# Four borders between stages of a two-block transformer: where gate products, a side projection and two sums stand, and one bank more

## The chip, the cores and the metric

One core of one Trainium2 chip runs the whole program. The metric is the device time of one execution in microseconds (us). TensorE (PE) multiplies matrices, VectorE (DVE) and ScalarE (ACT) do elementwise work, SyncE (SP) issues the weight transfers, GpSimd (POOL) does little here. Each engine runs its own queue of instructions in order and waits at an instruction until what that needs is there.

## What is computed

256 tokens of width 1024 pass two blocks. The first has a layer with gated linear attention (GLA) and one with stick-breaking attention, each with a squared-ReLU MLP and layer norms. The second has two layers of a mixed attention (forgetting and retention heads), a gated convolution FFN and a gated side input p. What the change touches, cut from the reference:

```python
q, k, v, g, a1 = jnp.split(x @ w_in, ...)                 # GLA mixer
log_a = jax.nn.log_sigmoid((a1 @ w_a2 + b_a)) / GATE_TAU   # its gates
b = jnp.cumsum(to_chunks(log_a), axis=3)
...
h = layer_norm(DEEPNORM_ALPHA * h + sq_relu_mlp(...), ...)  # end of the first block
u = rms_norm(h, attn_norm_w[i])                            # second block, i = 0, 1
...
u = rms_norm(h, ple_norm_w[i])
h = h + jax.nn.sigmoid(u @ w_ple_gate[i]) * (p[i] @ w_ple_proj[i])
...
return rms_norm(h, final_norm_w)
```

## The kernel before

All activations lie with the model width on the 128 partitions (8 blocks of 128) and the 256 tokens along the row. The products are float32 by two halves: a weight is split into a rounded part wh (ACT, L330) and a rest wl (DVE, L333), an activation into x0 and x1, and `mm3` writes three matmuls for one product, L402, L403 and L404, with 256 or 512 columns. In the trace x0, x1 and h are all called b, since they come from one pool of large tiles.

Weights stream through: `prep` writes one chunk of 128x1024 (512 KB), its transfer on SP into one of 4 buffers `raw`, its cast on ACT and its subtraction on DVE into one of 6 pairs wh, wl. Products accumulate in PSUM banks of two pools: `up` has 3 banks, `acc` 4, and one bank `aux` is for sums and spreads. A tile that takes a bank again waits until the last reader of the bank is done. Pools for small tiles (`sq`, `lnq`, `pleg`) have few buffers and wait in the same way.

The order of each queue is set when the program is built: a scheduler takes the instructions of all engines by priority, which follows the order in which the code is written, and by its own estimate of when each is ready. What is written later goes behind, casts of later weights slip in between, and the chip runs the queues as they then stand.

The four places of the change:

- The gates of GLA. `gla` projects v in two halves of 48 matmuls (`w_gv`, j = 0 and 1, 16 steps of three). `hooks` are pairs of a step and a function that is called there. `rank` (step 11 of the first half) makes the low rank a1 by 16 matmuls, then ACT and DVE split it (L755, L756, tile a). `gates` (step 14) multiplies it by w_a2 into two `acc` banks (8 matmuls, L764), then takes the log-sigmoid and the running sums: four ABS on ACT (L768), four DVE operations (L769), Exp and Ln over all (L396), a subtraction (L773), four scans (L775), a subtraction (L777), the rows `glagrow`, twelve `glaE` (L808), and `glaK`, `glaQ` (L819, L822), which the first GLA product (L829) needs. Between them PE has the second half of v and the q and k projections (`w_gqk`).
- The p projections. `ple_proj` makes both products with p, one per layer, between the last layer norm's sums and its application. Each has four blocks in an `up` bank, and each block has a copy to SBUF on ACT (L1243) and, at the end, a transfer to a DRAM buffer `prd`. The second one's blocks have six matmuls of 512 columns. `normed` then applies the norm: per pair of blocks lnq (DVE L618), h (L624), x0 (ACT L626), x1 (DVE L627), and squares on ACT with a running sum `ssum` on DVE (L642, L644).
- The first layer's gate (`ple`, L1249 to L1269). Four blocks of `w_pg0`; the last is done in two halves, (0,) and (1,), which lie in one bank. DVE multiplies each by the norm's factor (L1266), ACT takes the sigmoid, DVE multiplies by p's part (L1268) and adds h (L1269). Behind it come the squares for the next norm (L526, L527, L642), the projections w_rg and w_f of the next layer, with the sums over the partitions (L486, which needs ssum), the reciprocal root by Ln and Exp (rsv, rsa, rsr) and its spread over the tokens (diag, L495, and four matmuls L496).
- The last layer (`last`). `w_pg1` in 16 steps; at step 3 `stat` asks for the two sums (L486 and the root behind it), at step 7 `turn(1)` transposes the second half of h.

Of the kernel before, what the change touches and what calls it, by code (L numbers as in the profile page):

```python
# [10 lines left out]
F32 = mybir.dt.float32  # L11
F32R = mybir.dt.float32r
# [3 lines left out]
P = 128  # L16
T = 256
D = 1024
KB = D // P
# [194 lines left out]
KST, KSS, KPL, KRM, KSP = 5, 5, 1, 7, 3  # L214
# [5 lines left out]
class Net:  # L220
# [511 lines left out]
    def gla(self, x):  # L732
        nc = self.nc
# [54 lines left out]

        v = self.b8().rearrange("p a b -> p (a b)").rearrange("p (c n) -> p c n", c=2)
        for j in range(2):  # L790
            pv = self.proj_tok("w_gv", j, x, hooks=[(11, rank), (14, gates)] if j == 0 else ())
            for c in range(2):
                after = nc.scalar.copy(v[:, c, j * 512:(j + 1) * 512], pv[c].rearrange("p a b -> p (a b)")).ins
        dep = mybir.DependencyInfo(mybir.DependencyClass.NoSync, mybir.DependencyReason.DATA)
# [418 lines left out]
                prev = hid  # L1213
        return self.late(accs, lambda c: self.down(accs, nm, j0, prev, pn, False, True, [c]))

    def ple_proj(self, stats):

        nc = self.nc
        self.prd = []
        for l in range(2):  # L1220
            pr = self.b8()
            pt = self.t([P, 2, T], "ptin")
            i = nc.scalar.dma_start(pt, self.A["p"][l]).ins
            self.tc.add_manual_dep(i, self.mark.name, mybir.DependencyInfo(mybir.DependencyClass.NoSync, mybir.DependencyReason.DATA), reason="order")
            px = (self.t([P, 2, T], "ph", F32R), self.t([P, 2, T], "pl", F32R))
            self.split(px, slice(0, 2), pt)
            w, _ = self.w(f"w_pp{l}", 0)
            halves = self.ready[self.use - 1][2]
            for c in range(4):
                ps = self.pup()  # L1230
                if l == 0:
                    for i in range(2):
                        for k in range(2):
                            self.mm3(ps[:, i, :], *w((2 * c + i) * 2 + k), px[0][:, k, :], px[1][:, k, :],
                                     k == 0 and i == 0, k == 1)
                else:
                    cs, ns = slice(c // 2 * P, c // 2 * P + P), slice(c % 2 * 512, c % 2 * 512 + 512)
                    for k in range(2):
                        self.mm3(ps.rearrange("p a b -> p (a b)"), px[0][:, k, cs], px[1][:, k, cs],
                                 *(t[:, ns] for t in halves[k]), k == 0, k == 1)  # L1240
                if l == 0 and c == KPL:
                    stats()
                nc.scalar.copy(pr[:, 2 * c:2 * c + 2, :], ps)  # L1243
            d = self.dram.tile([P, 8, T], F32, name=f"prd{l}")
            nc.scalar.dma_start(d, pr)
            self.prd.append(d)

    def ple(self, l, h, x, acc):
        nc = self.nc  # L1249
        n = self.b8()  # L1250
        pr = self.b8()
        nc.scalar.dma_start(pr, self.prd[l])
        for c in range(4):
            w, _ = self.w(f"w_pg{l}", c)
            ps = self.pup()
            g = self.t([P, 2, T], "pleg")
            for os in (((0, 1),) if c < 3 else ((0,), (1,))):
                for k in range(KB):
                    for o in os:
                        self.mm3(ps[:, o, :], *w(2 * k + o), x[0][:, k, :], x[1][:, k, :], k == 0 and o == 0, k == KB - 1)  # L1260
                    if c == 0 and k == KRM:
                        R2 = self.rms_full(acc).unsqueeze(1).to_broadcast([P, 2, T])
                a, b = os[0], os[-1] + 1
                sl = slice(2 * c + a, 2 * c + b)
                gg = g[:, a:b, :]
                nc.vector.tensor_tensor(out=gg, in0=ps[:, a:b, :], in1=R2[:, a:b, :], op=ALU.mult)  # L1266
                self.act(gg, gg, "Sigmoid")
                nc.vector.tensor_tensor(out=gg, in0=gg, in1=pr[:, sl, :], op=ALU.mult)  # L1268
                nc.vector.tensor_tensor(out=n[:, sl, :], in0=gg, in1=h[:, sl, :], op=ALU.add)  # L1269
        return n  # L1270


    def last(self, h, x, acc):
        nc = self.nc
# [47 lines left out]
                q.dma_start(self.out[c * P:(c + 1) * P, i * 512:i * 512 + 512], yy)  # L1322

        turn(0)
        ps = self.proj_tok("w_pg1", 0, x, hooks=[(3, stat), (7, lambda: turn(1))])
        for c in range(2):
            leave(c, 0, 0, 512, flat(ps[c]), 3 * c)
        self.w("w_pg1", 2)
# [18 lines left out]
    def run(self):  # L1347
# [31 lines left out]
        for l in range(2):  # L1379
# [8 lines left out]
            ln = self.layer_norm(h, mix, f"ln_g{l}1", f"ln_b{l}1", l == 0)  # L1388
            if end(f"b{l}", lambda: (ln['stats'](), self.normed(ln))[1][0]):
                return  # L1390
        self.ple_proj(ln["stats"])
        h, x, acc = self.normed(ln, "an0")
        for l in range(2):
            if l == 1:
                x, acc = self.rms(h, f"an{l}")
            o, hooks = self.mix2(l, x, acc)
            h = self.residual(h, self.pairs(f"w_out{l}", o, hooks, 6))
            if end(f"c{l}", lambda: h):
                return
            x, acc = self.rms(h, f"fn{l}")  # L1400
            h = self.residual(h, self.ffn2(l, x, acc))
            if end(f"d{l}", lambda: h):
                return
            x, acc = self.rms(h, f"pn{l}")
            if l == 1:
                return self.last(h, x, acc)
            h = self.ple(l, h, x, acc)
            if end(f"e{l}", lambda: h):
                return
# [28 lines left out]
```

## Time and profile before

| | us |
|---|---|
| median of 3 runs | 1303.39 (1301.37 to 1304.65) |
| the profiled execution, own time | 1302.13 |
| its span | 1300.4 |
| PE busy in it | 1282.7 (99%) |
| DVE, ACT busy | 946.8 (73%), 750.8 (58%) |
| TensorE's granted clock, mean | 0.998 |

The span is what the profiler sees from the first to the last instruction; the rest of an execution lies around it. A row of a timeline gives the start, the length, the engine, the line, the operation with its output and inputs, and, in brackets, how long the engine was idle before it and what ended that. A run of equal instructions stands in one row with its count (x4), and the length is then that of the run. The ends of matmuls are modelled, so the pitch from start to start tells more than the length.

### The profile page before, as it was taken

Reading aid. Unit: us, or ns where it says so; the run is one execution under the profiler, and the core shown is the slowest. Engines: PE = TensorE matmul, PEld = TensorE weight load, DVE = VectorE, ACT = ScalarE, POOL = GpSimd, SP = SyncE. Lnnn points to the kernel's source line nnn. Section 1 sums busy time; section 2 is a strip of 40 time slices with the busy share of each in tenths; the row PEclk is TensorE's granted clock in tenths of the full one; section 3 lists DMA queues with packets and bytes.
Section 4 is the critical chain, followed back from the end, with each engine's and each line's share of the span. In section 5 each row is a group of like instructions: output and inputs, shape, how many; then the busy total and the mean of one; then the engine's idle time right before and its main releaser. Section 6 shows DMA issues by size and latency. Waiting matters only on the chain.

```text
span 1300.4 us, 25420 instructions
## 1 busy us (share of the span) xinstructions
PE 1282.7 (99%) x10314; PEld 1236.5 (95%) x10314; DVE 946.8 (73%) x1514; ACT 750.8 (58%) x1181; POOL 36.2 (3%) x89
## 2 busy tenths in 40 slices
PE   8999999999999999999999999999999999999997
PEld 6999999999899999999989999999989899999996
DVE  6979855559557955558887788766787869885755
ACT  6556744447776744446746665544674557554544
POOL 0000000000231000000010000000001000000000
PEclk9999999999999999999999999999999999999999
DMA  8654666654533575555654465565657446656561
GB/s 288 217 172 155 193 197 183 189 179 141 185 115 118 171 228 189 185 189 194 215 182 140 138 207 187 183 184 158 220 167 221 141 127 196 192 185 188 170 222 50
DMA packets 64694, 232.78 MB, mean 179 GB/s; under 512 B 7216, under 2 KB 7488, under 8 KB 63936
## 3 DMA queue, kind: packets, MB, share of 16 engines
q1 hardware_dynamic: 61920, 220.75, 54.1%
q10 hardware_dynamic: 2016, 8.28, 1.7%
q0 software_dynamic: 640, 2.11, 0.5%
q8 instruction: 81, 1.33, 0.4%
q14 instruction: 37, 0.30, 0.1%
HBM read 227.96 MB, written 3.16 MB: 178 GB/s over the span
## 4 chain that ended last, share of the span: by engine, by line
PE 90%; DVE 5%; DMA 3%; ACT 2%; issue 1%; POOL 0%; SPq 0%; POOLq 0%; ACTq 0%; DVEq 0%
PE up L402 20%; PE up L403 19%; PE up L404 19%; PE acc L403 9%; PE acc L404 8%; PE acc L402 8%; DVE wl L333 1%; DMA raw<-in_w_pg_dram 1%; PE aux L976 1%; ACT wh L330 1%; DMA wa<-in_w_a_dram 1%; PE aux L586 1%; PE acc L1128 1%; PE acc L1070 0%; DMA raw<-in_w_gv_dram 0%
## 5 line engine op out<-in xcount | busy, mean ns | idle before, releaser
L333 DVE TENSOR_TENSOR wl<-raw,wh 128x1024 fp32r<-128x1024 f32 (+2 forms) x420 | 506.3, 1210 | 257.1 <-ACT wh L330 255.4
L330 ACT CAST wh<-raw 128x1024 fp32r<-128x1024 f32 (+2 forms) x420 | 434.9, 1036 | 387.3 <-PE acc L403 139.2
L402 PE MATMUL up<-b,wh 128*128 128x256 f32 (+1 forms) x2032 | 576.2, 284 | 2.8 <-DVE pleg L1266 1.6
L403 PE MATMUL up<-b,wh 128*128 128x256 f32 (+1 forms) x2032 | 572.4, 282 | 0.2 <-DVE b L527 0.2
L404 PE MATMUL up<-b,wl 128*128 128x256 f32 (+1 forms) x2032 | 569.6, 280 | 0.0
L402 PEld LDWEIGHTS up<-b,wh 128*128 128x128 f32 x2032 | 381.5, 188 | 10.3 <-issue 5.2
L403 PEld LDWEIGHTS up<-b,wh 128*128 128x128 f32 x2032 | 382.8, 188 | 1.2 <-DVE b L527 0.4
L404 PEld LDWEIGHTS up<-b,wl 128*128 128x128 f32 x2032 | 382.9, 188 | 0.2 <-issue 0.2
L403 PE MATMUL acc<-b,wh 128*128 128x256 f32 (+1 forms) x960 | 270.6, 282 | 0.0
L404 PE MATMUL acc<-b,wl 128*128 128x256 f32 (+1 forms) x960 | 270.4, 282 | 0.0
L402 PE MATMUL acc<-b,wh 128*128 128x256 f32 (+1 forms) x960 | 270.2, 281 | 0.0
L402 PEld LDWEIGHTS acc<-b,wh 128*128 128x128 f32 x960 | 181.1, 189 | 0.1
L403 PEld LDWEIGHTS acc<-b,wh 128*128 128x128 f32 x960 | 181.0, 189 | 0.1
L404 PEld LDWEIGHTS acc<-b,wl 128*128 128x128 f32 x960 | 180.7, 188 | 0.1
L402 PE MATMUL up<-wh,b 128*128 128x512 f32 (+1 forms) x136 | 52.9, 393 | 1.6 <-ACT wh L361 1.6
L403 PE MATMUL up<-wl,b 128*128 128x512 f32 (+1 forms) x136 | 51.9, 381 | 0.0
L404 PE MATMUL up<-wh,b 128*128 128x512 f32 (+1 forms) x136 | 51.7, 381 | 0.0
L467 ACT CAST b<-ffny 128x256 fp32r<-128x256 f32 x44 | 17.9, 407 | 54.3 <-DVE ffny L1202 53.4
L402 PEld LDWEIGHTS up<-wh,b 128*128 128x128 f32 x136 | 25.5, 188 | 8.2 <-ACT wh L361 2.3
L404 PEld LDWEIGHTS up<-wh,b 128*128 128x128 f32 x136 | 25.5, 188 | 5.3
L403 PEld LDWEIGHTS up<-wl,b 128*128 128x128 f32 x136 | 25.6, 188 | 4.9 <-DVE wl L362 0.4
L1194 DVE TENSOR_TENSOR glaS<-up,rfr 128x256 f32<-128x256 f32 x44 | 18.7, 425 | 12.4 <-PE up L404 12.3
(257 smaller groups left out, 1151.3 us busy)
## 6 DMA issues: line engine op xcount, KB each, us to landing
raw<-in_w_fu_dram SPq DMA_DIRECT2D x88, 512.0 KB, 4.2
raw<-in_w_mu_dram SPq DMA_DIRECT2D x64, 512.0 KB, 4.1
raw<-in_w_md_dram SPq DMA_DIRECT2D x64, 512.0 KB, 4.2
raw<-in_w_fd_dram SPq DMA_DIRECT2D x32, 512.0 KB, 3.7
raw<-in_w_sqk_dram SPq DMA_DIRECT2D x16, 512.0 KB, 4.1
raw<-in_w_rqk_dram SPq DMA_DIRECT2D x16, 512.0 KB, 4.9
raw<-in_w_fqk_dram SPq DMA_DIRECT2D x16, 512.0 KB, 4.4
raw<-in_w_out_dram SPq DMA_DIRECT2D x16, 512.0 KB, 3.8
```

The source lines that it names most:

```text
L330: i = nc.scalar.copy(hi, r).ins
L333: i = nc.vector.tensor_tensor(out=lo, in0=r, in1=hi, op=ALU.subtract).ins
L402: mm(o, wh, xh, start=first, stop=False, skip_group_check=True)
L403: mm(o, wh, xl, start=False, stop=False, skip_group_check=True)
L404: self.last_mm = mm(o, wl, xh, start=False, stop=last, skip_group_check=True).ins
L467: nc.scalar.copy(out[0][:, i, :], src)
L586: nc.tensor.matmul(ps[:, k, :], ones, s[k][:, i, :], start=(k == 0 and i == 0), stop=(i == 1), skip_group_check=True)
L976: self.nc.tensor.matmul(pO[r, i // 2, :], v[:, 0, hc], ws[i][:, 0:256], start=(i < 2), stop=False, skip_group_check=True)
L1128: mm(pls[i][:, a:b], qk[r, 0, a:a + P], qk[r, 1, 0:b - a], start=(a == 0), stop=True, skip_group_check=True)
L1194: nc.vector.tensor_tensor(out=a[:, 2:], in0=ps[:, 0, :], in1=R, op=ALU.mult)
```

## The change

Four edits, all of where something is written or which bank it takes; no product, sum or transfer is added or left out. `gates` moves from step 14 of the first half of v to step 1 of the second, nine matmuls later. `ple_proj` is cut into `ple_load` (transfer, split, weights) and `ple_proj` (products, copies, transfer out), and the second projection's part is written behind `normed`. The last half block of `ple` takes an `acc` bank instead of the second half of the `up` bank. In `last` the sums are asked for at step 10 instead of step 3.

```diff
-            pv = self.proj_tok("w_gv", j, x, hooks=[(11, rank), (14, gates)] if j == 0 else ())
+            pv = self.proj_tok("w_gv", j, x, hooks=[(11, rank)] if j == 0 else [(1, gates)])
...
-    def ple_proj(self, stats):
...
-        for l in range(2):
-            pr = self.b8()
...
+    def ple_load(self, l):
+        nc = self.nc
+        pr = self.b8()
...
+        return l, pr, px, w, halves
+
+    def ple_proj(self, l, pr, px, w, halves, stats=None):
+
+        nc = self.nc
+        if l == 0:
+            self.prd = []
+        for c in range(4):
+            ps = self.pup()
...
+            nc.scalar.copy(pr[:, 2 * c:2 * c + 2, :], ps)
+        d = self.dram.tile([P, 8, T], F32, name=f"prd{l}")
+        nc.scalar.dma_start(d, pr)
+        self.prd.append(d)
...
-            ps = self.pup()
             g = self.t([P, 2, T], "pleg")
             for os in (((0, 1),) if c < 3 else ((0,), (1,))):
+                ps = self.pacc() if os == (1,) else self.pup()
                 for k in range(KB):
                     for o in os:
-                        self.mm3(ps[:, o, :], *w(2 * k + o), x[0][:, k, :], x[1][:, k, :], k == 0 and o == 0, k == KB - 1)
+                        self.mm3(ps[:, o, :], *w(2 * k + o), x[0][:, k, :], x[1][:, k, :], k == 0 and o == os[0], k == KB - 1)
...
-        ps = self.proj_tok("w_pg1", 0, x, hooks=[(3, stat), (7, lambda: turn(1))])
+        ps = self.proj_tok("w_pg1", 0, x, hooks=[(7, lambda: turn(1)), (10, stat)])
...
-        self.ple_proj(ln["stats"])
+        pp = self.ple_load(0)
+        self.ple_proj(*pp, stats=ln["stats"])
+        pp = self.ple_load(1)
         h, x, acc = self.normed(ln, "an0")
+        self.ple_proj(*pp)
```

The queues of SP and POOL keep their order. ACT's queue at the gates, in the kernel before, from the split of a1 on (wh of raw: a cast of w_gv's or w_gqk's weights; acc to b: an ABS; up to b: a copy of v):

```order
L755 CAST a_22_154<-aux_235 128x256
L330 CAST wh_177<-raw_175 128x1024
L330 CAST wh_183<-raw_181 128x1024
L768 ACTIVATE b_20_152<-acc_255,vec 128x256
L768 ACTIVATE b_20_152<-acc_264,vec 128x256
L793 COPY b_25_160<-up_161 128x512
L768 ACTIVATE b_20_152<-acc_255,vec 128x256
L768 ACTIVATE b_20_152<-acc_264,vec 128x256
L793 COPY b_25_160<-up_162 128x512
L396 ACTIVATE b_20_152<-b_20_152 128x1024
L330 CAST wh_213<-raw_211 128x1024
L396 ACTIVATE b_20_152<-b_20_152 128x1024
```

The same stretch in the changed kernel:

```order
L755 CAST a_22_154<-aux_235 128x256
L330 CAST wh_177<-raw_175 128x1024
L793 COPY b_25_160<-up_161 128x512
L330 CAST wh_183<-raw_181 128x1024
L793 COPY b_25_160<-up_162 128x512
L768 ACTIVATE b_20_152<-acc_280,vec 128x256
L330 CAST wh_213<-raw_211 128x1024
L768 ACTIVATE b_20_152<-acc_280,vec 128x256
L768 ACTIVATE b_20_152<-acc_289,vec 128x256
L330 CAST wh_219<-raw_217 128x1024
L330 CAST wh_264<-raw_262 128x1024
L768 ACTIVATE b_20_152<-acc_289,vec 128x256
```

The four ABS stood among two copies of v, ahead of the casts that follow them; now three casts (wh_213, wh_219, wh_264, all of w_gqk) stand between the first and the last of them, and a fourth (wh_270) between Exp and the Ln, which is the next row.

ACT's queue at the second p projection, before, from the last copy of the first projection on (up_7242 to up_7266 are the second projection's four blocks):

```order
L1243 COPY b_1040_7123<-up_7207 128x512
L1243 COPY b_1060_7223<-up_7242 128x512
L1245 DMA prd_7221<-b_1040_7123 128x2048
L1243 COPY b_1060_7223<-up_7250 128x512
L1243 COPY b_1060_7223<-up_7258 128x512
L1243 COPY b_1060_7223<-up_7266 128x512
L626 ACTIVATE b_1075_7277<-lnq_7283,gw_7280 128x256
L1245 DMA prd_7274<-b_1060_7223 128x2048
L626 ACTIVATE b_1075_7277<-lnq_7283,gw_7280 128x256
L626 ACTIVATE b_1075_7277<-lnq_7291,gw_7280 128x256
L642 ACTIVATE ssum_7279<-b_1074_7276 128x256
```

And in the changed kernel, where these blocks are up_7303, up_7311 and on:

```order
L1247 COPY b_1040_7123<-up_7207 128x512
L1249 DMA prd_7221<-b_1040_7123 128x2048
L626 ACTIVATE b_1071_7243<-lnq_7249,gw_7246 128x256 x2
L626 ACTIVATE b_1071_7243<-lnq_7257,gw_7246 128x256
L642 ACTIVATE ssum_7245<-b_1070_7242 128x256
L626 ACTIVATE b_1071_7243<-lnq_7257,gw_7246 128x256
L642 ACTIVATE sq_7266<-b_1070_7242 128x256
L642 ACTIVATE sq_7274<-b_1070_7242 128x256
L626 ACTIVATE b_1071_7243<-lnq_7269,gw_7246 128x256 x2
L642 ACTIVATE sq_7280<-b_1070_7242 128x256
L642 ACTIVATE sq_7288<-b_1070_7242 128x256
L1247 COPY b_1060_7223<-up_7303 128x512
```

The first copy of the second projection followed the last one of the first directly; now six L626 and five squares (L642, the first of them into ssum) stand between.

PE's queue in the last block of the first layer's gate, before, where the first half ends (up_11377) and w_rg0's products (up_11488) begin:

```order
L403 MATMUL up_11377<-b_1631_11111,wh_11162 128x256
L404 MATMUL up_11377<-b_1630_11110,wl_11163 128x256
L402 MATMUL up_11488<-b_1678_11435,wh_11235 128x256
L403 MATMUL up_11488<-b_1679_11436,wh_11235 128x256
L404 MATMUL up_11488<-b_1678_11435,wl_11236 128x256
```

And in the changed kernel:

```order
L403 MATMUL up_11378<-b_1631_11111,wh_11162 128x256
L404 MATMUL up_11378<-b_1630_11110,wl_11163 128x256
L402 MATMUL acc_11407<-b_1630_11110,wh_11156 128x256
L403 MATMUL acc_11407<-b_1631_11111,wh_11156 128x256
L404 MATMUL acc_11407<-b_1630_11110,wl_11157 128x256
```

Twelve products of w_rg0 stood between the halves of the block; now the second half, in its own bank (acc_11407), follows the first, and all of w_rg0 comes behind it.

## Rows read from the trace of the kernel before

**Rows 1.** The page's busy time by engine.

```profile
PE 1282.7 (99%) x10314; PEld 1236.5 (95%) x10314; DVE 946.8 (73%) x1514; ACT 750.8 (58%) x1181; POOL 36.2 (3%) x89
```

**Rows 2.** PE's waits: waiting operation, releaser, us in total, times, longest.

```profile
PE up L402 <- DVE pleg L1266: 1.6, 1, 1.6
PE aux L486 <- DVE ssum L644: 1.5, 1, 1.5
...
PE aux L496 <- DVE diag L495: 1.2, 1, 1.2
```

**Rows 3.** Timeline of PE at the gates (start, us, then as described above).

```profile
19.49 1.56 PE L764 MATMUL acc<-a,w 128*128 128x256 f32 x8 [0.68 <-ACT a L755]
20.89 0.39 PE L402 MATMUL up<-wh,b 128*128 128x512 f32 x1
...
40.37 0.29 PE L403 MATMUL up<-b,wh 128*128 128x256 f32 x1
40.49 0.28 PE L404 MATMUL up<-b,wl 128*128 128x256 f32 x1
40.70 0.86 PE L829 MATMUL acc<-glaQ,glaK 128*64 128x256 f32 x8
```

**Rows 4.** Timeline of ACT there: two casts of w_gqk that wait for their transfer.

```profile
28.04 1.05 ACT L330 CAST wh<-raw 128x1024 fp32r<-128x1024 f32 x1 [0.29 <-DMA raw<-in_w_gqk_dram]
30.63 1.05 ACT L330 CAST wh<-raw 128x1024 fp32r<-128x1024 f32 x1 [1.54 <-DMA raw<-in_w_gqk_dram]
```

**Rows 5.** Timeline of DVE there: the scans and two wl.

```profile
29.30 2.44 DVE L775 TENSOR_TENSOR_SCAN b<-tab,b 128x256 f32<-128x256 f32 x4
...
37.23 2.36 DVE L333 TENSOR_TENSOR wl<-raw,wh 128x1024 fp32r<-128x1024 f32 x2
```

**Rows 6.** Timeline of PE at the second p projection: its fourth block, then w_rg0.

```profile
611.60 0.39 PE L402 MATMUL up<-wh,ph 128*128 128x512 f32 x1
...
612.74 0.39 PE L404 MATMUL up<-wh,pl 128*128 128x512 f32 x1
614.30 0.50 PE L402 MATMUL up<-b,wh 128*128 128x256 f32 x2 [1.17 <-ACT b L626]
```

**Rows 7.** Timeline of ACT there: a copy, then L626 and squares.

```profile
613.16 0.59 ACT L1243 COPY b<-up 128x512 f32<-128x512 f32 x1 [0.77 <-PE up L404]
...
615.47 0.59 ACT L626 ACTIVATE b<-lnq,gw 128x256 fp32r<-128x256 f32 x1
615.96 0.40 ACT L642 ACTIVATE sq<-b 128x256 f32<-128x256 f32 x1
616.26 0.59 ACT L626 ACTIVATE b<-lnq,gw 128x256 fp32r<-128x256 f32 x1
```

**Rows 8.** Timeline of DVE there: the first two lnq and the third.

```profile
611.21 1.28 DVE L618 TENSOR_TENSOR lnq<-b,rfr 128x512 f32<-128x512 f32 x2
...
615.20 0.69 DVE L618 TENSOR_TENSOR lnq<-b,rfr 128x512 f32<-128x512 f32 x1
```

**Rows 9.** PE's last matmul, and busy time by stretch: PE, PEld, DVE, ACT, POOL, clock.

```profile
1292.49 0.28 PE L404 MATMUL up<-wh,b 128*128 128x256 f32 x1
1294.00:1296.00 2.00, 0.00 (x0) 0.00 (x0) 0.96 (x3) 0.51 (x2) 0.72 (x2) 0.89 0.00 1
1296.00:1298.00 2.00, 0.00 (x0) 0.00 (x0) 0.49 (x1) 0.72 (x1) 0.02 (x1) 0.50 0.29 109
```

**Rows 10.** Timelines of PE and ACT at the gate's last block and w_rg0.

```profile
951.59 0.39 PE L402 MATMUL up<-b,wh 128*128 128x256 f32 x1 [1.59 <-DVE pleg L1266]
...
955.64 1.28 ACT L390 ACT_TABLE_LOAD   x1
...
958.08 0.75 PE L402 MATMUL up<-b,wh 128*128 128x256 f32 x2
...
962.38 1.05 ACT L330 CAST wh<-raw 128x1024 fp32r<-128x1024 f32 x1 [3.67 <-DMA raw<-in_w_rv_dram]
```

**Rows 11.** Timeline of ACT in the last layer: the first sigmoid.

```profile
1280.10 0.69 ACT L396 ACTIVATE pleg<-up,rsr 128x512 f32<-128x512 f32 x1 [2.38 <-PE up L404]
```

More of the change, by code (lines that the diff above doesn't have):

```diff
@@ L1214, in ffn2 @@
         return self.late(accs, lambda c: self.down(accs, nm, j0, prev, pn, False, True, [c]))
-    def ple_proj(self, stats):
+    def ple_load(self, l):
         nc = self.nc
-        self.prd = []
-        for l in range(2):
-            pr = self.b8()
[L1222 to L1229, printed above, removed]
-                ps = self.pup()
[L1231 to L1237, printed above, removed]
-                    for k in range(2):
[L1239 to L1246, printed above, removed]
@@ new lines, in ple_load @@
+        pr = self.b8()
+        pt = self.t([P, 2, T], "ptin")
+        i = nc.scalar.dma_start(pt, self.A["p"][l]).ins
+        self.tc.add_manual_dep(i, self.mark.name, mybir.DependencyInfo(mybir.DependencyClass.NoSync, mybir.DependencyReason.DATA), reason="order")
+        px = (self.t([P, 2, T], "ph", F32R), self.t([P, 2, T], "pl", F32R))
+        self.split(px, slice(0, 2), pt)
+        w, _ = self.w(f"w_pp{l}", 0)
+        halves = self.ready[self.use - 1][2]
+        return l, pr, px, w, halves
@@ new lines, in ple_proj @@
+    def ple_proj(self, l, pr, px, w, halves, stats=None):
[4 more added lines that the diff above has]
+            ps = self.pup()
+            if l == 0:
+                for i in range(2):
+                    for k in range(2):
+                        self.mm3(ps[:, i, :], *w((2 * c + i) * 2 + k), px[0][:, k, :], px[1][:, k, :],
+                                 k == 0 and i == 0, k == 1)
+            else:
+                cs, ns = slice(c // 2 * P, c // 2 * P + P), slice(c % 2 * 512, c % 2 * 512 + 512)
+                for k in range(2):
+                    self.mm3(ps.rearrange("p a b -> p (a b)"), px[0][:, k, cs], px[1][:, k, cs],
+                             *(t[:, ns] for t in halves[k]), k == 0, k == 1)
+            if l == 0 and c == KPL:
+                stats()
+            nc.scalar.copy(pr[:, 2 * c:2 * c + 2, :], ps)
+        d = self.dram.tile([P, 8, T], F32, name=f"prd{l}")
+        nc.scalar.dma_start(d, pr)
+        self.prd.append(d)
@@ L1254, in ple @@
             w, _ = self.w(f"w_pg{l}", c)
-            ps = self.pup()
             g = self.t([P, 2, T], "pleg")
             for os in (((0, 1),) if c < 3 else ((0,), (1,))):
+                ps = self.pacc() if os == (1,) else self.pup()
                 for k in range(KB):
                     for o in os:
-                        self.mm3(ps[:, o, :], *w(2 * k + o), x[0][:, k, :], x[1][:, k, :], k == 0 and o == 0, k == KB - 1)
+                        self.mm3(ps[:, o, :], *w(2 * k + o), x[0][:, k, :], x[1][:, k, :], k == 0 and o == os[0], k == KB - 1)
                     if c == 0 and k == KRM:
```

## The prediction

> **What bounds the kernel now.** I read the head of the page first: TensorE (PE) is busy for 1282.7 us, 99% of the span of 1300.4 [rows 1]. So the span is PE's work, which the change leaves alone (the same matmuls, in another order at three borders), and some 17.7 us in which PE stands still. Only that idle time can be won, and only new idle time can be lost. The list of PE's waits says where it lies: five of its ten lines belong to the places that the diff touches. Call these places A (gates: 0.68 for ACT's a [rows 3]), B (second p projection: 1.17 for ACT's L626 [rows 6]), C (last block of the first gate and the norm behind it: pleg 1.6 and diag 1.2) and D (two sums in the last layer: ssum 1.5) [rows 2]. After that I read the timelines of PE, ACT and DVE around each place, and held them against the new order of each queue. The profiled execution took 1302.13 us, 1.73 more than its span and 1.26 under the median of 1303.39. All terms are differences within that one execution, and I put their sum on the median.
>
> **A, the gates, nine matmuls later.** PE's wait before the gate products goes: 0.68 us ahead of them, and inside them 20.89 - 19.49 = 1.40 us for eight products that at a pitch of 0.118 need 0.94, so 0.46 more; together 1.1 [rows 3]. The casts of a (ACT and DVE) end near 19.9, and the products now start near 20.7. But what the gates issue behind them also moves. The first of it are four ABS on ACT, and the new order puts three casts of w_gqk weights between the first and the last of them. In the rows of before the third of these casts waits for its transfer until 28.04, and the fourth, which now stands between Exp and Ln, until 30.63 [rows 4]. Earlier PE frees none of the raw buffers that these transfers use (DVE does, with wl), so I keep the landings. Then: third cast 28.04 to 29.0, the last ABS to 29.4, Exp to 30.5, the fourth cast 30.6 to 31.6, Ln to 32.6. On DVE the wl of that cast (1.2) ends at 32.8, the subtraction L773 at 33.9, one more wl at 35.0. From the scans at 29.30 to the first GLA product L829 at 40.70 it took 11.4 us, in which three wl stood (a pair took 2.36, so 3.5), of which none stands there now: 7.9 remain [rows 5]. So L829 starts at about 43.0 instead of 40.70. Nothing hid this chain before: the last product ahead of L829 started at 40.49, so there were about 0.1 us of slack [rows 3]. Net of A: +2.3, though PE reaches the place 1.1 earlier; it then idles from 39.5 to 43.0, 3.5 us. Bounds: -1.1 if the chain is hidden after all, +3.0 if the landings slip by as much as the fourth waited beyond the third.
>
> **B, the second p projection behind the norm.** PE's queue still has its four blocks of six products ahead of w_rg0, but ACT's copies of them now stand behind most of the norm. The pool of the blocks has three banks, so the fourth block writes the bank of the first and starts when that has been copied. Before, each copy ran at once, and the fourth block started at 611.60 [rows 6, 7]. Now ACT has six L626 and five squares to run ahead of the first copy. The first L626 can start when lnq is there, about 611.9 [rows 8]. With 0.49 per L626 and 0.30 per square [rows 7] that is 2.9 + 1.5 = 4.4 us, to 616.3; the third lnq, which came at 615.20 before and has to come before the last two L626, and the h behind the squares add 0 to 1.1 us, of which I take 1.0. The copy takes 0.59 and runs 617.4 to 618.0, and PE idles from 611.6 to 618.0. The fourth block (1.37) then ends at 619.4, and w_rg0 starts there instead of 614.30. The 1.17 us that it waited for the first L626 is already in this. Net of B: +5.0, bounds +4.0 and +5.4. What follows is in step with it: ACT's queue from the first copy to the last square holds about 4 us of work, so the sums for the norm are ready near 622.5, and PE asks for them 48 matmuls after 619.4, at 625.1.
>
> A rule of the Trainium skill (Perfetto Trace Analysis, section Matmuls) speaks for PE being untouched here: independent groups that rotate through PSUM banks let ACT empty one while PE fills the next. In the rows of before the copy does follow its block by 0.03 us [rows 6, 7]; by the rule B would be -1.2, by the queue it is +5.0.
>
> **The clock after such a wait.** The rows show that idle PE loses its clock: the last matmul of the program starts at 1292.49, and the granted clock is a mean of 0.89 in 1294 to 1296 and 0.50 behind it. That is 1.56 us at full and the rest at half, so it fell from 2.4 to 1.2 GHz at 1295.6, 2.8 us after that matmul ended [rows 9]. The gaps of before were all under 2 us, and the clock stayed up. B's 6.4 us are well above 2.8. No row shows how it comes back. The lower bound is 0 (with the first matmul). The one stretch at 1.2 GHz that rows show lasted 4.8 us, from 1295.6 to the end; matmuls that run so long at half pace lose 2.4 us, and I take that, since nothing shows a quick return. A's 3.5 us are also above 2.8, but so little that I leave a second 2.4 out of the sum and in the range.
>
> The Trainium skill (TensorE: Matmul & The Clock Gate, Part 1) says that "the default state is throttled, and activity releases the throttle". That speaks against the 0: by it the sum is the one with this term, and no row here shows the return.
>
> **C, a bank of its own for the gate's last block.** Its second half no longer waits until DVE has read the first half out of the same bank: the wait of 1.6 goes, and w_rg0 is no longer split around it. The wait for diag (1.2) goes too: rsa and rsr stood behind a cast that waited 3.67 us for w_rv, and that cast is now behind them [rows 2, 10]. Against it: the second half, which ran 24 matmuls from 951.59 to about 954.5, now follows the first without the wait (1.75 with its edges) and without twelve products of w_rg0 (1.4) between them, and ends near 951.3. So PE comes to the last eighth of w_rg0 42 matmuls later, at 956.3, while the last block's sigmoid and the table load (1.28) still stand before the last x. There PE stood about 0.5 us (the pair at 958.08 takes 0.75 instead of 0.28), and I expect 1.3 to 1.4 [rows 10]. Net of C: -2.8 + 0.9 = -1.9, bounds -2.8 and -0.3 (if what the two waits gave is spent on x).
>
> **D, the two sums asked for later.** PE waited 1.5 us for ssum; now the sums are asked for 15 products and 3.5 us later, when ssum is 2 us old. The new risk is the sigmoid behind it. PE ended the block near 1280.1, and ACT had by then waited 2.38 us [rows 11]. Now PE ends at about 1278.6 and the sums come at 1276.0; with rsv, rsa, rsr (0.2 each) and the table load of 1.28 (as in [rows 10]) ACT is ready at 1278.0. Net of D: -1.5, bounds -1.5 and 0.
>
> **The sum.** 2.3 + 5.0 - 1.9 - 1.5 = +3.9, and with the clock in B +6.3 us. On the median that is 1309.7; the profiled execution would show about 1308.4.
>
> **Rivals.**
> 1. The clock does not matter (it comes back with the first matmuls, or the low stretch falls on time that PE would wait anyhow). For it: the last row at 1.2 GHz has no work in it, so nothing there shows a lasting loss. Against it: B's idle time is more than twice the 2.8 us, and behind it PE waits for nothing. +3.9, so 1307.3.
> 2. The clock falls in A also. For it: 3.5 is over 2.8. Against it: by 0.7 only, and one fall is all that was seen. +8.7, so 1312.1.
> 3. The banks' rotation hides the copies after all, as the rule above has it. Place: the copy of B's first block; it decides from the point where that copy ends by 611.6. Against it: eleven instructions stand before it, each with a row. 2.3 - 1.2 - 1.9 - 1.5 = -2.3, so 1301.1.
> 4. On the other side: ACT's queue has slack at both borders, because the chunks of w_gqk land earlier than their rows say and B's copies are not late. It decides if the third cast at A ends by 25.5 instead of 29.0. Then only the removed waits count: -1.1 - 1.2 - 1.9 - 1.5 = -5.7, so 1297.7. For it is only that all five waits are really in the rows; against it, that the transfers have landing times that PE does not set.
>
> **How the numbers follow.** My forecast has 0.44, rival 1 0.23, rival 2 0.23, rival 3 0.06, rival 4 0.04. A measurement of this kernel can tell about 0.3% from no change, 3.9 us, so faster is below 1299.5 and slower above 1307.3. Rival 4 is faster: 0.04. Rival 3 and half of rival 1, which lies on the border, are the same: 0.06 + 0.12 = 0.18. The rest is slower, 0.78. The likeliest case gives 1309.7. Below it, rival 1 with C at its good bound gives 1306.4, and with B at its low one too 1305.4; above it rival 2 gives 1312.1, and with A at its high bound 1312.8. So 1305 to 1313 holds the forecast and rivals 1 and 2 but for their corners, about 8 in 10.
>
> **What would show it.** In the changed kernel's list of PE's waits: a wait for ACT's copy (now L1247) of about 6.4 us near 612 and a wait of about 3.5 us before L829, both new; no wait for a (L755), for ssum, for diag in the first layer behind C, or for pleg. A window of 8 us after B's fourth block should show a granted clock well under 1, and one after L829 nearly 1. ACT's last ABS should start near 29.0, with a wait for a w_gqk transfer just before it. In C, PE should wait about 1.3 us near the last eighth of w_rg0. I am wrong if the first copy of B runs before the L626 rows, if L829 starts before 41 us, or if the time comes out below 1303.

## The result, and the profile after

The changed kernel takes 1309.79 us (median of 5 runs, 1309.07 to 1312.36) against 1303.39 (5 runs, 1301.37 to 1304.65). The ratio is 1.0052 with a 95% interval of 1.0041 to 1.0064: 6.8 us slower, between 5.3 and 8.3. The medians differ by 6.4.

Its profiled execution was the slowest of the five, 1312.36 us with a span of 1310.6, while that of before, 1302.13, was one of the quicker ones. The two spans therefore differ by 10.2 us, more than the medians do, and the rows below have to be read place by place. PE's busy time and the list of what it waited for, in the changed kernel (waiting operation, releaser, us in total, times, longest):

```profile
PE 1287.1 (98%) x10314; PEld 1241.1 (95%) x10314; DVE 947.1 (72%) x1514; ACT 750.8 (57%) x1181; POOL 35.4 (3%) x89
...
PE up L402 <- ACT b L1247: 6.2, 1, 6.2
PE acc L829 <- DVE glaQ L822: 3.2, 1, 3.2
PE up L403 <- DVE b L527: 2.6, 3, 1.5
```

The first line answers to [rows 1]: PE is 4.4 us busier with the same 10314 instructions, so some of them ran slower. The waits of [rows 2] for pleg, ssum and diag are all gone, and so are those for ACT's a [rows 3] and for L626 [rows 6]. Two larger ones are there instead, 6.2 for a copy of the second p projection and 3.2 for the first GLA product.

At the gates, ACT and then PE in the changed kernel (the rows that answer to [rows 4] and [rows 3]):

```profile
28.13 1.05 ACT L330 CAST wh<-raw 128x1024 fp32r<-128x1024 f32 x1 [0.26 <-DMA raw<-in_w_gqk_dram]
29.09 0.46 ACT L768 ACTIVATE b<-acc,vec 128x256 f32<-128x256 f32 x1
```

```profile
42.76 1.38 PE L829 MATMUL acc<-glaQ,glaK 128*64 128x256 f32 x8 [3.19 <-DVE glaQ L822]
```

The third cast waits for its transfer as before, the last ABS stands right behind it, and L829 starts at 42.76 instead of 40.70.

At the second p projection, ACT and PE (answering to [rows 7] and [rows 6]; everything here lies 3.0 us later than before because of the gates):

```profile
618.59 1.09 ACT L626 ACTIVATE b<-lnq,gw 128x256 fp32r<-128x256 f32 x2 [0.69 <-DVE lnq L618]
619.59 0.81 ACT L642 ACTIVATE sq<-b 128x256 f32<-128x256 f32 x2
620.30 1.05 ACT L1247 COPY b<-up 128x512 f32<-128x512 f32 x2
```

```profile
614.36 0.39 PE L404 MATMUL up<-wh,pl 128*128 128x512 f32 x1
620.92 0.80 PE L402 MATMUL up<-wh,ph 128*128 128x512 f32 x1 [6.18 <-ACT b L1247]
621.52 0.63 PE L403 MATMUL up<-wl,ph 128*128 128x512 f32 x1
621.95 0.63 PE L404 MATMUL up<-wh,pl 128*128 128x512 f32 x1
```

The copies run behind six L626 and five squares, and behind a wait of 0.69 for DVE's third lnq. The products behind the wait come at a pitch of 0.43 where 0.23 was usual. Busy time by stretch says why (us, then PE, PEld, DVE, ACT, POOL with their counts, the granted clock, DMA share, GB/s), at both waits of the changed kernel:

```profile
42.00:44.00 2.00, 1.24 (x8) 1.07 (x8) 1.97 (x9) 1.93 (x3) 0.00 (x0) 0.76 0.01 4
44.00:46.00 2.00, 2.00 (x12) 1.94 (x10) 1.94 (x6) 2.00 (x3) 0.00 (x0) 0.50 0.03 8
46.00:48.00 2.00, 2.00 (x17) 2.00 (x17) 2.00 (x4) 1.32 (x2) 0.00 (x0) 0.89 0.23 35
...
618.00:620.00 2.00, 0.00 (x0) 0.00 (x0) 2.00 (x6) 1.41 (x4) 0.00 (x0) 0.97 0.06 25
620.00:622.00 2.00, 1.07 (x3) 0.89 (x4) 2.00 (x6) 2.00 (x5) 0.00 (x0) 0.50 0.00 0
...
624.00:626.00 2.00, 2.00 (x11) 2.00 (x10) 1.90 (x5) 1.41 (x3) 0.00 (x0) 0.50 0.39 156
626.00:628.00 2.00, 2.00 (x16) 2.00 (x16) 0.23 (x1) 0.07 (x1) 0.00 (x0) 0.82 0.99 272
```

The clock fell to 1.2 GHz near 619.9 (a mean of 0.97 over two us means that 0.12 us of them were at half) and came back near 626.7, so PE worked for 5.8 us at half pace, 2.9 us lost. At the gates it was at 1.2 GHz from about 43.0 to 46.4.

At the gate's last block and w_rg0 behind it, PE waits twice in the changed kernel:

```profile
970.78 0.38 PE L402 MATMUL up<-b,wh 128*128 128x256 f32 x1 [0.23 <-ACT b L526]
971.90 0.39 PE L403 MATMUL up<-b,wh 128*128 128x256 f32 x1 [0.74 <-DVE b L527]
```

Holding the starts of the same product numbers of both traces against each other gives a ledger: the gates +3.4 (2.1 of wait and 1.3 of slow products), the second p projection +7.6, the gate's last block -1.7, the sums -1.8; together +7.5. The other 2.7 us of the spans' 10.2 lie where nothing was changed. The larger piece, 2.0, is at the first block of w_pg0, where ACT's cast waited longer for its transfer in this execution:

```profile
939.62 1.05 ACT L330 CAST wh<-raw 128x1024 fp32r<-128x1024 f32 x1 [5.17 <-DMA raw<-in_w_pg_dram]
```

Before, that wait was 3.19 (925.84). In the profiles of the experiments below, the same stretch takes from 0.3 us less to 1.3 us more than before, so this piece differs from one profile to the next. A second piece does not. From one product near 714 us to one near 881 us the kernel before needs 166.8 us, and the kernel with the second p projection's move alone needs 167.8 (in each pair of rows the start of the first and of the last product):

```profile
714.13 0.49 PE L1149 MATMUL acc<-tab,foxl 128*128 128x128 f32 x3
...
880.95 0.28 PE L404 MATMUL up<-b,wl 128*128 128x256 f32 x1
```

```profile
723.74 0.49 PE L1149 MATMUL acc<-tab,foxl 128*128 128x128 f32 x3
...
891.53 0.28 PE L404 MATMUL up<-b,wl 128*128 128x256 f32 x1
```

All seven profiles with the whole second projection behind the norm have this 1.0 to 1.1 us, the kernel with the gates alone has 0.5, and the other five kernels have at most 0.1. So it comes with the program and is a part of what that move costs, though nothing of this stretch was edited, and no run here shows why. In the other direction, 0.7 us comes back between 68 and 260 us in all five profiles with the gates moved, and the cause of that is open too.

### The profile page after: what moved, and what is told of

Its sections match the earlier page's. It is cut to its first block, busy times and chain, and to the rows that moved or that the text cites. A ratio compares the mean times of both kernels' runs of the same rounds, so it can differ in the third digit from the quotient of the medians.

```text
span 1310.6 us, 25420 instructions
## 1 busy us (share of the span) xinstructions
PE 1287.1 (98%) x10314; PEld 1241.1 (95%) x10314; DVE 947.1 (72%) x1514; ACT 750.8 (57%) x1181; POOL 35.4 (3%) x89
## 4 chain that ended last, share of the span: by engine, by line
PE 89%; DVE 5%; DMA 3%; ACT 2%; issue 1%; POOL 0%; SPq 0%; POOLq 0%; ACTq 0%; DVEq 0%
PE up L402 19%; PE up L403 19%; PE up L404 19%; PE acc L403 9%; PE acc L402 9%; PE acc L404 9%; DVE wl L333 1%; PE aux L976 1%; DMA raw<-in_w_pg_dram 1%; DMA wa<-in_w_a_dram 1%; ACT wh L330 1%; PE aux L586 1%; PE acc L1128 1%; PE acc L1070 0%; DMA raw<-in_w_gv_dram 0%
## 5 line engine op out<-in xcount | busy, mean ns | idle before, releaser
L403 PE MATMUL up<-wl,b 128*128 128x512 f32 (+1 forms) x136 | 51.9, 381 | 0.0
```

The costliest lines, as they stand in the source:

```text
L403: mm(o, wh, xl, start=False, stop=False, skip_group_check=True)
```

## The experiments

Each was timed beside the kernel before on the same chip. In us on before, with the 95% interval of the ratio times 1303.4:

| kernel | ratio | us on before |
|---|---|---|
| changed kernel | 1.0052 | +6.8 (5.3 to 8.3) |
| gates alone | 1.0011 | +1.4 (0.1 to 2.7) |
| p projection alone | 1.0062 | +8.1 (6.5 to 9.8) |
| own bank alone | 0.9985 | -2.0 (-3.1 to -0.7) |
| later sums alone | 0.9979 | -2.7 (-4.0 to -1.6) |
| changed, p wait filled | 1.0031 | +4.0 (2.7 to 5.3) |
| changed, both waits filled | 1.0028 | +3.6 (2.3 to 4.8) |
| changed, p blocks in acc banks | 1.0012 | +1.6 (0.0 to 3.3) |
| the same, gates as before | 1.0003 | +0.4 (-1.2 to 2.0) |
| own bank and later sums | 0.9956 | -5.7 (-7.3 to -4.0) |
| those, p cut three and one | 0.9964 | -4.7 (-6.4 to -3.0) |
| before, wait for the sums filled | 1.0004 | +0.5 (-1.0 to 2.1) |
| p in acc banks, copies on DVE, gates as before | 1.0011 | +1.4 (-0.1 to 3.1) |

**One edit at a time.** Each kernel is the one before with one of the four edits.

The gates:

```diff
-            pv = self.proj_tok("w_gv", j, x, hooks=[(11, rank), (14, gates)] if j == 0 else ())
+            pv = self.proj_tok("w_gv", j, x, hooks=[(11, rank)] if j == 0 else [(1, gates)])
```

> The kernel before with the gates moved alone. Theory (ACT's last ABS waits behind a cast whose transfer lands near 28, and the clock falls while PE waits at L829): +2 us of wait and about 1.2 us of matmuls at 1.2 GHz, +3.3 us, 1306.7 on the median of before. Rival (the wait at the gates was the cost, the chain behind it has slack): -1.1 us, 1302.3.

+1.4 us. The sign is the theory's, but the interval excludes its +3.3 as well as the rival's -1.1. In its profile L829 starts at 43.02 after a wait of 2.00, and the clock is at half from about 44.6 to 48:

```profile
43.02 0.93 PE L829 MATMUL acc<-glaQ,glaK 128*64 128x256 f32 x8 [2.00 <-DVE glaQ L822]
```

```profile
44.00:46.00 2.00, 2.00 (x12) 2.00 (x13) 1.96 (x7) 2.00 (x4) 0.00 (x0) 0.64 0.04 8
46.00:48.00 2.00, 2.00 (x12) 2.00 (x11) 2.00 (x4) 1.59 (x2) 0.00 (x0) 0.51 0.20 23
```

So the place behaves as the theory has it. Part of the 3.3 us is not lost for good: in the same profile the wait for diag 900 us later is 0.3 instead of 1.2 [rows 2]. That wait hangs on a weight transfer, but that the one pays for the other was not tried. And the profile of before is a quick one here: in the nine profiles with the gates in their old place L829 starts at 40.56 to 41.60 (the middle one at 41.08), in the five with the gates moved at 42.76 to 43.90 (the middle one at 43.02), so the middles are 1.9 us apart. The rest of the gap between +3.3 and +1.4 stays open.

The second p projection (the whole of that part of the diff, with the rest as before):

```diff
-        self.ple_proj(ln["stats"])
+        pp = self.ple_load(0)
+        self.ple_proj(*pp, stats=ln["stats"])
+        pp = self.ple_load(1)
         h, x, acc = self.normed(ln, "an0")
+        self.ple_proj(*pp)
```

> The kernel before with the second p projection behind the norm alone. Theory (its fourth block waits for ACT's late copy of the first, and the clock falls meanwhile): +5 us of wait and about 2.5 to 3 us at 1.2 GHz, +7.7 us, 1311.1. Rival (the late copy alone, the clock costs nothing): +5 us, 1308.4. Second rival (what it was meant for, no wait for L626): -1.2 us, 1302.2.

+8.1 us, as the theory with the clock has it; its interval excludes both rivals. PE's longest wait in its profile is again this copy's:

```profile
PE up L402 <- ACT b L1247: 6.2, 1, 6.2
```

The own bank:

```diff
-            ps = self.pup()
...
+                ps = self.pacc() if os == (1,) else self.pup()
...
```

> The kernel before with the own bank for the gate's last half block alone. Theory: the waits for pleg and diag (1.6 and 1.2) go, some 0.9 us come at the last x of w_rg0: -1.9 us, 1301.5. Rival (what is won is waited for again at x): -0.3 us, 1303.1.

-2.0 us; the rival's -0.3 lies outside the interval. This profile holds something else as well. At the last layer, which this kernel leaves alone, PE waited 1.90 for ssum, and the clock fell:

```profile
1272.34 0.61 PE L486 MATMUL aux<-tab,ssum 128*128 128x1 f32 x4 [1.90 <-DVE ssum L644]
```

```profile
1272.00:1274.00 2.00, 1.67 (x7) 1.47 (x8) 2.00 (x3) 0.15 (x1) 0.00 (x0) 0.70 0.01 4
...
1276.00:1278.00 2.00, 2.00 (x13) 1.77 (x12) 1.17 (x2) 1.95 (x4) 0.00 (x0) 0.94 0.00 0
```

The later sums:

```diff
-        ps = self.proj_tok("w_pg1", 0, x, hooks=[(3, stat), (7, lambda: turn(1))])
+        ps = self.proj_tok("w_pg1", 0, x, hooks=[(7, lambda: turn(1)), (10, stat)])
```

> The kernel before with the two sums of the last layer asked for at step 10 alone. Theory: the wait for ssum goes and ACT's root is ready before the sigmoid: -1.5 us, 1301.9. Rival (the sigmoid now waits for the root): 0, 1303.4.

-2.7 us, more than the 1.5 that the wait took in the profile of before. The wait is gone and nothing stands in its place. Why it is worth more is taken up below.

The four singles add to +1.4 + 8.1 - 2.0 - 2.7 = +4.8, just under the interval of the whole (5.3 to 8.3). Each single has an interval of its own of 1.2 to 1.7 us to either side, so no difference between the sum and the whole is shown.

**What the clock costs.** To keep PE at work during the wait of the second p projection, this kernel puts products of a tile of zeros ahead of its fourth block:

```diff
+                if c == 3:
+                    self.fill(12)
...
+    def fill(self, n):
+        pw = self.pacc()
+        for k in range(n):
+            i = self.nc.tensor.matmul(pw[:, 0, :], self.idle[:, 0:P], self.idle, start=True, stop=True).ins
...
```

> The changed kernel with twelve extra products of a tile of zeros (128x256, 0.47 us each, never read) in PE's queue ahead of the fourth block of the second p projection, so that PE works through most of its 6.2 us of waiting. Theory (the clock falls in that wait and its return costs PE 3 us): no stretch below full clock there, -3.0 us against the changed kernel, +3.4 on before. Rival (the wait is all, the clock costs nothing): 0 against the changed kernel, +6.4 on before.

+4.0 against +6.8: 2.7 us came back, though the fourth block started when it did before (620.77 and 620.92). In its profile PE works through the wait and the clock is 1.00 throughout:

```profile
614.43 5.34 PE L1219 MATMUL acc<-idle 128*128 128x256 f32 x24
...
620.77 0.50 PE L402 MATMUL up<-wh,ph 128*128 128x512 f32 x1 [0.99 <-ACT b L1257]
```

```profile
620.00:622.00 2.00, 1.23 (x5) 1.05 (x6) 2.00 (x6) 2.00 (x6) 0.00 (x0) 1.00 0.00 0
```

The two intervals touch, but the traces agree with the times: the 340 products around this place (602.9 to 653.6 before, 50.7 us) take 58.3 us in the changed kernel and 56.0 in this one. So useless work made the program faster, and the clock's share of the p projection's cost is shown: 2.4 to 2.7 of about 8. The next kernel fills the gates' wait as well:

```diff
+            if j == 0:
+                self.fill(6)
             pS = self.pacc().rearrange("p a b -> p (a b)")
```

> As the one with twelve extra products, and six more ahead of the first GLA product, in PE's wait of 3.2 us there. Theory: the clock stays up at both places, another -1.2 us, +2.2 on before. Rival (what the clock costs at GLA is waited for later anyhow, since the gates alone measured only +1.4): no further gain, +3.4 on before.

+3.6 against +4.0: no further gain that can be measured, but the run does not show the rival's reason. In the profile with only the p wait filled, a wait of 2.7 us at L829 did not bring the clock down at all, so there was nothing to win back in it. And the filling moved another queue. DVE behind the first GLA products, with the p wait filled and then with both filled:

```profile
45.28 1.06 DVE L834 TENSOR_TENSOR glaS<-acc,tab 64x384 f32<-64x384 f32 x3
```

```profile
45.29 2.35 DVE L333 TENSOR_TENSOR wl<-raw,wh 128x1024 fp32r<-128x1024 f32 x2
47.56 1.06 DVE L836 TENSOR_TENSOR glaS<-acc,tab 64x384 f32<-64x384 f32 x3
```

Two wl now stand ahead of glaS (L834 there, L836 here), and PE waits for it:

```profile
PE acc L844 <- DVE glaS L836: 0.9, 1, 0.9
```

What a fall of the clock costs here is better read from the four profiles with the gates moved and this wait unfilled. The 400 products from the first L829 on take 51.9 and 52.0 us in the two where the clock fell (the changed kernel, the gates alone) and 50.8 in the two where it stayed up (p wait filled, p blocks in acc banks): 1.1 to 1.2 us.

**Mending the second p projection.** Its four blocks take the four acc banks, so that none waits for a copy:

```diff
-            ps = self.pup()
+            ps = self.pacc() if l == 1 else self.pup()
```

> The changed kernel with the second p projection's four blocks in the four acc banks instead of three up banks, all else as it is. Theory (the bank of the first block was the wait): no wait for L1247, no low clock there, and L626 is no longer waited for, so the p part gives -1.2 instead of +8.1; with the gates' +1.4, the bank's -2.0 and the sums' -2.7 that is -4.5 on before, ratio 0.9965. Rival (ACT is late as such: six copies and squares ahead of the last L626 make w_rg0 wait for its last x): 2 to 3 us of it come back, -2 on before.

+1.6 us: better than the changed kernel by 5.2, but far from -4.5. The next one also puts the gates back:

```diff
-            pv = self.proj_tok("w_gv", j, x, hooks=[(11, rank)] if j == 0 else [(1, gates)])
+            pv = self.proj_tok("w_gv", j, x, hooks=[(11, rank), (14, gates)] if j == 0 else ())
```

> As the one with acc banks, with the gates back at step 14 of the first half. Theory (moving the gates gains nothing, because the chain behind them ends no earlier): -1.2 - 2.0 - 2.7 = -5.9 on before, ratio 0.9955, and 1.4 us faster than the one with acc banks alone. Rival (the gates' move does pay in company with the other edits): slower than that one by 1 us.

+0.4 us; the theory's -5.9 is refuted, and the 1.2 us by which it beats the one with acc banks alone can't be told from none at these intervals. The waits for L626 and for the copies are really gone (0.6 for L627 is left). In their place, 45 us on, the retention products wait, and the clock falls behind them. PE, DVE and ACT in this kernel:

```profile
660.59 2.00 PE L1070 MATMUL acc<-rot,rot 32*128 32x256 f32 x32 [3.00 <-DVE rot L1060]
```

```profile
655.26 1.38 DVE L333 TENSOR_TENSOR wl<-raw,wh 128x1024 fp32r<-128x1024 f32 x1 [1.28 <-ACT wh L330]
...
658.97 1.23 DVE L333 TENSOR_TENSOR wl<-raw,wh 128x1024 fp32r<-128x1024 f32 x1 [1.13 <-ACT wh L330]
660.11 0.75 DVE L1060 TENSOR_TENSOR rot<-rot,retb 128x256 f32<-128x256 f32 x2
```

```profile
654.18 1.05 ACT L330 CAST wh<-raw 128x1024 fp32r<-128x1024 f32 x1 [4.75 <-DMA raw<-in_w_fv_dram]
```

```profile
662.00:664.00 2.00, 2.00 (x19) 1.78 (x16) 1.41 (x7) 0.01 (x1) 0.00 (x0) 0.50 0.97 213
```

The rot that PE needs stands on DVE behind two wl that wait for ACT's casts. ACT now waits for weight transfers, 4.75 us for one, where in the kernel before it waited mostly for PE to free a pair of weight tiles. In the queue of before three of the four casts of w_rv stood ahead of rsr, in the new one none does; a raw buffer that is cast later takes its next transfer later. SP's queue shows this: the four transfers of w_fv begin to be issued at 641.55 in the kernel before and at 645.96 in this one, although PE was at the same products then to within 0.3 us (the rows are SP's, each with the time from its first to its last issue):

```profile
641.55 9.58 SPq L325 DMA_DIRECT2D raw<-in_w_fv_dram  x4
```

```profile
645.96 8.38 SPq L325 DMA_DIRECT2D raw<-in_w_fv_dram  x4
```

By the starts of the same products the place costs 4.6 us, 3.0 of wait and the rest slow products. With the 1.0 us between 714 and 881 us that is 5.6 of the 6.3 us that the theory missed.

To tell whether the casts' place on ACT is the cause, the same kernel with the copies on DVE:

```diff
-            nc.scalar.copy(pr[:, 2 * c:2 * c + 2, :], ps)
+            (nc.vector.tensor_copy if l == 1 else nc.scalar.copy)(pr[:, 2 * c:2 * c + 2, :], ps)
```

> As the one with acc banks and the gates as before, with the four copies of the second p projection on DVE instead of ACT, which puts two casts of w_rv ahead of the norm's reciprocal root on ACT again (three stood there before, none with the copies on ACT). Theory (the late casts on ACT made the weight transfers late, and so the wait of 3 us at L1070): the wait at L1070 goes, -4 to -6 on before. Rival (the 2.4 us of copies only change the engine: now DVE's wl are late, and the transfers with them): the wait at L1070 stays, about 0 on before.

+1.4 us, so the theory that ACT's casts alone are it falls. The wait at L1070 is 3.4, and w_fv is issued as late as with the copies on ACT (645.96):

```profile
PE acc L1070 <- DVE rot L1060: 3.4, 1, 3.4
```

```profile
623.24 1.29 DVE L1247 COPY b<-acc 128x512 f32<-128x512 f32 x2
...
624.50 3.56 DVE L333 TENSOR_TENSOR wl<-raw,wh 128x512 fp32r<-128x512 f32 x4
```

```profile
645.65 9.57 SPq L325 DMA_DIRECT2D raw<-in_w_fv_dram  x4
```

The rival's outcome holds: now four wl stand behind the copies on DVE, and a raw buffer is free only after its wl. On either engine the copies behind the norm stand ahead of the weights' preparation, and the transfers start late. That the one makes the other late is read from the order of the queues; no run put the casts and wl back in their places and left the copies.

**What is left.** The own bank and the later sums without the other two:

```diff
-            ps = self.pup()
...
+                ps = self.pacc() if os == (1,) else self.pup()
...
-        ps = self.proj_tok("w_pg1", 0, x, hooks=[(3, stat), (7, lambda: turn(1))])
+        ps = self.proj_tok("w_pg1", 0, x, hooks=[(7, lambda: turn(1)), (10, stat)])
```

> The kernel before with the own bank and the later sums, without the gates' and the p projection's moves. Theory (the two gains are at places 300 us apart and add): -2.0 - 2.7 = -4.7 us on before, ratio 0.9964. Rival (PE ahead by 2 us at the first runs into later transfers before the second): -2.7.

-5.7 us, 1299.31 in the median against 1304.94: faster than both kernels. The two gains add, since -4.7 lies in the interval and the rival's -2.7 does not. Then, on top, the second p projection cut so that only its fourth block stands behind the norm (the diff is against the changed kernel):

```diff
...
+        self.ple_proj(*pp, cs4=range(3))
         h, x, acc = self.normed(ln, "an0")
-        self.ple_proj(*pp)
+        self.ple_proj(*pp, cs4=range(3, 4))
```

> As the one with bank and sums, with the second p projection cut: three blocks and their copies ahead of the norm as before, the fourth block's product and copy behind it, so that its bank (the first block's) is free in time and one copy alone stands behind the norm's squares. Theory (only one copy has to leave ACT's way for L626): the wait of 1.2 for L626 goes, -5.9 on before, ratio 0.9955. Rival (any copy behind the norm pushes the casts of w_rv back and the retention products wait, as with the acc banks): -4.7 or worse, with a wait for rot at L1070.

-4.7 us, no gain over -5.7. There is no wait for rot, so the rival's mechanism is not what happened, but the wait of 1.2 for L626 was replaced by one for L627:

```profile
PE up L403 <- DVE b L627: 0.8, 1, 0.8
```

By the starts of the products behind it, 0.6 us was won there. But the clock fell in that profile from 959.6 to 963.0, behind waits of 0.23 and 0.74 us in w_rg0, and that stretch takes 1.5 us longer than with bank and sums alone. Whether the cut pays where the clock stays up was not shown.

Last, the kernel before with three zero products in the wait for the sums:

```diff
         def stat():
...
+            pw = self.paux()
+            for k in range(3):
+                i = nc.tensor.matmul(pw[:, 0, :], self.idle[:, 0:P], self.idle, start=True, stop=True).ins
...
```

> The kernel before with three extra products of a tile of zeros (0.47 us each, never read) ahead of the two sums in the last layer, in PE's wait of 1.5 us. Theory (even so short a wait lets the clock fall in some executions, which is why the later sums measured -2.7 where the wait is 1.5): no low stretch there, -1 us on before. Rival (the wait alone): 0.

+0.5 (-1.0 to 2.1): the theory's -1 is not borne out, and the run does not settle it. In its profile the clock stayed at 1.00, as in the profile of before, and PE did the extra products and still waited:

```profile
1271.92 1.46 PE L1298 MATMUL aux<-idle 128*128 128x256 f32 x6
...
1275.03 0.58 PE L486 MATMUL aux<-tab,ssum 128*128 128x1 f32 x4 [1.43 <-DVE ssum L644]
```

The filling also moved the sums: they stand five products earlier in PE's queue than before, so at a pitch of 0.23 PE had 1.2 us less of its own work ahead of them.

## Why the prediction was right

The forecast was 1309.7 us and the measured median is 1309.79, and the sign and the places hold, with the second p projection as by far the largest term. Term by term it is less exact than the sum:

- **Gates, +2.3.** The mechanism is right to the row: the last ABS behind the third cast (29.09, worked out 29.0) and L829 at 42.76 (worked out 43.0). Alone the edit measured +1.4. That no second term for the clock belongs into the sum was right in the outcome, but not for the reason given: the clock did fall there, in two of the four profiles with the gates moved and that wait unfilled, and cost 1.1 to 1.2 us where it fell. Two things that the prediction did not see make the move cheaper: the 0.7 us that comes back by 260 us, and that L829 starts later in other executions without the move than in the profile of before.
- **Second p projection, +5.0 and 2.4 for the clock.** The copy started at 620.30; worked out was 617.4, which with the 3.0 us that all lies later there is 620.4. The wait is 6.2 where 6.4 was worked out. Alone, +8.1 against 7.4; the filled wait gives the clock's part as 2.4 to 2.7 against 2.4. The 1.0 us between 714 and 881 us, for which the sum has no term, is in the 8.1 too. The clock's term rested on one stretch without any work in it [rows 9] and came out near partly by luck: in the changed kernel the clock stayed low for 5.8 us of work, where the row had 4.8 us of idling.
- **Own bank, -1.9.** -2.0 alone, -1.7 by the starts of the products. The waits at the last x of w_rg0 add to 1.0 in the changed kernel's profile, worked out 1.3 to 1.4.
- **Later sums, -1.5.** -2.7 alone (1.6 to 4.0 faster), so this term was mis-sized. The step that failed is taking the wait's length from one profile. By the starts of the same products the move gains 1.8 to 2.1 us against the profile of before in all nine profiles that have it, and that profile has a short wait: in three others it was 1.53, 1.78 and 1.90, the last with a fallen clock behind it. The sums wait for squares and casts that hang on a transfer of w_pg, and the two waits grow together: ACT's was 2.92 in the profile of before, and 3.13, 3.27 and 3.34 in those three. How often the clock falls there was not counted.
- **The rivals.** That the clock would not matter is refuted by the filled wait, and with it the bound of 0 for that term: the clock stayed low for 5.8 us after PE went on, so the end of the wait alone did not bring it back. The Trainium skill (TensorE: Matmul & The Clock Gate, Part 1), by which "activity releases the throttle", agrees with that. That the clock falls at the gates too, the second rival, happened in some executions, at half the price that the prediction gave it. That the banks' rotation hides the copies failed with three banks: the copy that empties the first stood behind eleven other instructions on ACT, and PE waited 6.2 us. With four banks no product waited for a copy, and then the weights' preparation was late. That rotation is a rule of the Trainium skill's Perfetto Trace Analysis (section Matmuls), and these traces agree with it for four banks and not for three.

The profiled execution was forecast at about 1308.4 us and took 1312.36. Of the 3.9 us between the forecast and the measured difference to the profile of before, the four places have 1.2 (+7.5 in the ledger against +6.3), and 2.7 lie where the prediction had no term.

Against the times of the singles, the terms' errors are -0.9 at the gates, +0.7 at the p projection, -0.1 at the bank and -1.2 at the sums, -1.5 in all: the singles add to 4.8 where 6.3 was forecast and 6.4 to 6.8 measured for the whole. With about 1.3 us of uncertainty on each single that gap can't be told from none, and that the total hit to a tenth is chance.

## What to carry to other kernels

Moving work behind something in the code moves every instruction that it issues, on every engine: four blocks of products, moved to get L626 out earlier, put their copies behind eleven others on ACT, and PE paid through a bank; with banks enough, it paid 45 us later through the weight transfers. Read the new order of the queue that empties the banks before believing that a wait is gone, and look at the weight casts in it too, since they are what the transfers wait for. And when PE must wait, price the clock behind the wait as well as the wait. A filler is an edit like any other: at the gates and at the sums it moved what stands in the queues, and the result was no answer to the question.

## What the runs showed of the hardware

- The clock's fall adds to the wait. A wait of 6.2 us took TensorE from 2.4 to 1.2 GHz in both profiles that have it unfilled, and cost 2.4 to 2.7 us of later work; products of zeros in the wait kept it up and won that back.
- The prediction held a wait against the 2.8 us of [rows 9]. The runs show falls after shorter ones: after 1.90 us in the last layer (own bank alone), and near the start of four programs, where PE waits 1.6 to 1.9 us for its first weights and the clock is then at 0.50 to 0.75 between 8 and 12 us; in the kernel before the same wait of 1.61 left it at 1.00. After 1.8 and 2.7 us at L829 it stayed up in two profiles, after 2.0 and 3.2 it fell in two others. No row here tells which it will be. Behind the shorter waits the fall came when PE was at work again: 0.3 us after L829 started in the changed kernel, 1.5 us after it in the gates alone, 0.5 us after the sums in the last layer. The low stretches lasted 3.4 us in the last layer and at the gates (43.0 to 46.4), 6.8 us at the p projection.
